# First stage of a decoder-block kernel in a written order, with aligned tiles and a sink column

## The chip, the cores and the metric

One core of one Trainium2 chip runs the whole program. The metric is the device time in microseconds (us) from launch to end, the median of the runs shown. Five engines run side by side, each in its own fixed order of instructions: PE (TensorE, the matmuls), PEld (its weight loads, shown apart), DVE (VectorE), ACT (ScalarE) and POOL (GpSimd). SP issues the DMAs. Semaphores hold an instruction until what it needs is there, and everything behind it on its engine waits with it.

## What is computed

One layer of a decoder block on 512 tokens of width 1024, in float32:

```python
h = rmsnorm(x, norm_mix)
proj = h @ w_in                       # 13 parts: q, k, v of two mixers, gates
# mixer A: window of 128 keys, and a sink logit per head in the softmax
logits = where(valid, q @ k * scale + bias, NEG)
probs = softmax(concatenate([logits, sink_col], axis=-1))[..., :span]
y_A = probs @ v
# mixer B: a compressed, a selected and a window branch, weighed by gates
x = x + (sigmoid(gA) * (y_A @ w_up_a) + sigmoid(gB) * (y_B @ w_up_b)) @ w_out
x = x + ConvFFN(rmsnorm(x, norm_ffn))
out = rmsnorm(x, norm_final)
```

## The kernel before

Every product is made of three matmuls: a float32 matrix is split in a high part (a cast, on ACT) and a low part (source minus high part, a two-input subtraction on DVE or POOL; `split`, L78), and high times high, high times low and low times high are summed (`three`, L90). A weight of 128x1024 goes through `weight` (L82): a DMA into `raw` (three buffers), the cast and the subtraction into `hl` (three buffers). The sets `POOLJ`, `U1J` and `WOP` name the weights whose subtraction is POOL's.

**First stage** (L96 to L195). The four token tiles `x` and two halves of the value weights `wvr` (816 KB each) are loaded by SP. The norm's row `nmix` is spread over the partitions by float32 matmuls into `gam`. For each tile t, `norm_x` takes two squares on ACT (L156), a sum and a scale on DVE, the power on POOL (L137), scales the tile by `r` and `gam` (L161), transposes it on PE (`tp_x`, L144), and splits it into `xTh` and `xTl`. `values(t)` sums 24 matmuls of 408 columns into `v` (L177), splits the result into `VA` and `VB`, and takes the gates. There are 96 such matmuls. The order on each engine is a scheduler's: weights of later jobs (`hl_ka`, `hl_qa`), and the bias rows `pg` (L421, for the tables `TA` and `TB`), stand between the first stage's instructions.

**Mixer A** (`unit_a`, L475; eight units: four token tiles, two groups). Per unit: four times two `scores` matmuls, a DVE pass that adds the bias from `TA` and takes the negative maximum `nma` (L449), a minimum with the negative sink (L491), four exponentials on ACT that also sum (`sma`), the sink's own exponential (`esa`, L494 and L495), its addition to the sum (L496), a reciprocal, and the scaling of `Pa` (three of four heads on POOL, L505). Then transposes (`pT`), splits (`pth`, `ptl`) and value matmuls (`oa`). Between these steps `fill` places matmuls of a queue of jobs: projections such as `p_ka`, `p_qa`, `p_ksl` (24 matmuls of 512 columns each), and the compressed branch's `h`. A job's result leaves PSUM before the second next job may start (`mm` has two banks), by DVE and ACT: `QA`, `QB`, `cx`, `KS`.

**After that** come mixer B with gate jobs `p_ga` and `p_gb` (145 to 338 us), the merge, the output projection, and the FFN (`ug`, `fo`), which is matmuls nearly alone.

`TA` is loaded from a DRAM copy `gdr` of the bias rows, which one DMA writes from 8 partitions, 32 copies each (L423).

Of the kernel before, what the change touches and what calls it, by code (L numbers as in the profile page):

```python
# [49 lines left out]
def hybrid(tc, x, wv, wblk, w1, w2, wua, wub, wout, wfi, wfo, nmix, nffn, nfin, sinks, par, table, onehot, out):  # L50
# [9 lines left out]
    with es:  # L60
        C = es.enter_context(tc.tile_pool(name="const", bufs=1))
        SL = es.enter_context(tc.tile_pool(name="slots", bufs=1))
        WR = es.enter_context(tc.tile_pool(name="wring", bufs=3))
# [39 lines left out]
        for h in range(2):  # L103
            sl = slice(h * 512, (h + 1) * 512)
            nc.sync.dma_start(xt[0][:, sl], x[0:P, sl])
            if h == 0:
                nc.sync.dma_start(grow[:, :D], nmix)
        ones = grow[:, D:]
        V.memset(ones, 1.0)
        gam = [bank("sc", f"gam{h}") for h in range(2)]  # L110
        for h in range(2):
            T.matmul(gam[h], ones, grow[:, h * 512 : (h + 1) * 512], start=True, stop=True)
# [764 lines left out]
```

## Time and profile before

| | us |
|---|---|
| median of 3 runs (770.99 to 771.98) | 771.27 |
| profiled execution, its own time | 771.21 |
| its span, first to last instruction | 769.4 |
| PE busy in the span | 747.5 (97%) |
| DVE, ACT, POOL busy | 451.0, 369.4, 156.8 |
| first matmul of `p_ka` (end of the first stage) | 38.7 |
| first matmul of `p_ga` | 145.0 |

In a row of the timeline the first number is the start in us from the span's start, the second the length; then engine, line, operation, output<-inputs, partitions x elements, a count, and in brackets the idle time of the engine before it with what ended it. PEld rows start where a matmul's weights are loaded, so four in a row give the step from matmul to matmul. In a row by stretch, each engine has its busy time and a count; behind them stand the mean granted clock of TensorE (1.00 is 2.4 GHz, 0.50 is 1.2 GHz) and the share and rate of the DMAs. In a group's row the numbers behind the bar are busy us and mean ns of one.

### The profile page before, as it was taken

The numbers are of one execution on the slowest core, as the hardware profiler recorded it, in microseconds if no ns is written. First come the engines' busy times: TensorE is split into PE (matmuls) and PEld (weight loads), VectorE is DVE, ScalarE is ACT, GpSimd is POOL, SyncE is SP. The second block draws the span as 40 slices with busy tenths as digits, with TensorE's granted clock in tenths as the row PEclk, the third lists the DMA queues.
The fourth block names the chain that finished last, engine by engine and source line by source line (L and its number), as shares of the span: only waits on it lengthen the run. The fifth ranks groups of instructions, "written<-read, shape, count | busy, mean of one in ns | idle before, by whom it ended". The sixth has DMA issues, their size and how long they took to land.

```text
span 769.4 us, 9745 instructions
## 1 busy us (share of the span) xinstructions
PE 747.5 (97%) x3590; PEld 623.3 (81%) x3590; DVE 451.0 (59%) x921; ACT 369.4 (48%) x692; POOL 156.8 (20%) x134
## 2 busy tenths in 40 slices
PE   7999989999999999999999999999999999999996
PEld 5788778788888888878889888888888888888885
DVE  5537988747655578759465665665556564214123
ACT  7345685745655856665344434343434443113213
POOL 5023536325333444402400000000000000002001
PEclk9999998999999999999999999999999999999999
DMA  8463335421112112405321323232322324232302
GB/s 304 98 148 111 108 93 169 126 83 55 56 55 83 55 60 69 145 1 192 111 78 60 109 83 110 82 110 89 104 92 101 102 90 136 85 107 85 107 28 109
DMA packets 24182, 76.74 MB, mean 100 GB/s; under 512 B 3748, under 2 KB 4900, under 8 KB 24134
## 3 DMA queue, kind: packets, MB, share of 16 engines
q1 hardware_dynamic: 24134, 76.12, 31.2%
q8 instruction: 28, 0.46, 0.3%
q14 instruction: 20, 0.16, 0.1%
HBM read 72.96 MB, written 3.15 MB: 99 GB/s over the span
## 4 chain that ended last, share of the span: by engine, by line
PE 89%; DVE 6%; issue 1%; POOL 1%; ACT 1%; DMA 1%; SPq 0%; POOLq 0%; DVEq 0%; ACTq 0%
PE ug L91 10%; PE ug L92 10%; PE ug L93 10%; PE fo L772 5%; PE fo L771 5%; PE fo L770 5%; PE pT L456 3%; PE up L91 2%; PE p_gb L91 2%; PE p_gb L92 2%; PE p_gb L93 2%; PE up L93 2%; PE up L92 2%; PE wo L91 2%; PE wo L92 2%; PE wo L93 2%
## 5 line engine op out<-in xcount | busy, mean ns | idle before, releaser
L92 PE MATMUL ug<-hTl,hl_fi 128*128 128x512 f32 (+1 forms) x376 | 141.1, 375 | 0.0
L93 PE MATMUL ug<-hTh,hl_fi 128*128 128x512 f32 (+1 forms) x376 | 141.1, 375 | 0.0
L91 PE MATMUL ug<-hTh,hl_fi 128*128 128x512 f32 (+1 forms) x376 | 140.9, 376 | 0.0
L93 PEld LDWEIGHTS ug<-hTh,hl_fi 128*128 128x128 f32 x376 | 70.8, 188 | 12.9
L91 PEld LDWEIGHTS ug<-hTh,hl_fi 128*128 128x128 f32 x376 | 70.6, 188 | 12.9
L92 PEld LDWEIGHTS ug<-hTl,hl_fi 128*128 128x128 f32 x376 | 70.8, 188 | 12.6
L754 ACT ACTIVATE cv<-ug,prm 128x512 f32<-128x512 f32 x44 | 34.3, 780 | 96.2 <-PE ug L93 96.2
L755 DVE SCALAR_TENSOR_TENSOR cv<-ug,prm,cv 128x511 f32<-128x511 f32 x44 | 33.0, 750 | 77.1 <-ACT cv L754 77.0
L771 PE MATMUL fo<-hl_fo,AH 128*128 128x512 f32 x176 | 68.8, 391 | 0.0
L770 PE MATMUL fo<-hl_fo,AH 128*128 128x512 f32 x176 | 67.3, 389 | 0.0
L796 POOL TENSOR_TENSOR X<-X,nfin 128x512 f32<-128x512 f32 x4 | 5.2, 1319 | 297.0 <-ACT junk L794 297.0
L80 DVE TENSOR_TENSOR hl_fo<-raw_fo,hl_fo 128x1024 fp32r<-128x1024 f32 x22 | 27.1, 1235 | 64.7 <-ACT hl_fo L79 64.7
L79 ACT CAST hl_fo<-raw_fo 128x1024 fp32r<-128x1024 f32 x22 | 23.1, 1052 | 65.8 <-PE fo L772 65.8
L80 DVE TENSOR_TENSOR hl_fi<-raw_fi,hl_fi 128x1024 fp32r<-128x1024 f32 x44 | 53.5, 1217 | 1.8 <-ACT hl_fi L79 1.8
L772 PE MATMUL fo<-hl_fo,AL 128*128 128x512 f32 x128 | 49.8, 389 | 0.0
L80 DVE TENSOR_TENSOR ptl<-pT,pth 128x512 fp32r<-128x512 f32 x54 | 36.5, 685 | 19.0 <-ACT pth L79 9.9
L378 ACT ACTIVATE Pb<-Pb,nmb 128x512 f32<-128x512 f32 (+3 forms) x64 | 35.9, 562 | 23.9 <-DVE nmb L449 23.6
L79 ACT CAST hl_fi<-raw_fi 128x1024 fp32r<-128x1024 f32 x44 | 45.5, 1037 | 2.4 <-PE wo L93 2.4
L79 ACT CAST pth<-pT 128x512 fp32r<-128x512 f32 x54 | 30.9, 587 | 17.7 <-PE ob L611 8.2
L771 PEld LDWEIGHTS fo<-hl_fo,AH 128*128 128x128 f32 x176 | 33.0, 188 | 7.2
L770 PEld LDWEIGHTS fo<-hl_fo,AH 128*128 128x128 f32 x176 | 33.0, 188 | 7.1
L449 DVE CUSTOM_DVE_ANT_0 Pb<-scores,TB 128x512 f32<-128x512 f32 (+3 forms) x64 | 30.7, 486 | 11.1 <-PE scores L445 9.2
(313 smaller groups left out, 1730.0 us busy)
## 6 DMA issues: line engine op xcount, KB each, us to landing
raw_fi<-in_wfi_dram SPq DMA_DIRECT2D x44, 512.0 KB, 3.3
raw_fo<-in_wfo_dram SPq DMA_DIRECT2D x22, 512.0 KB, 3.3
raw_w<-in_w_dram SPq DMA_DIRECT2D x8, 512.0 KB, 3.8
raw_ga<-in_wblk_dram SPq DMA_DIRECT2D x8, 512.0 KB, 3.3
raw_gb<-in_wblk_dram SPq DMA_DIRECT2D x8, 512.0 KB, 3.2
raw_wo<-in_wout_dram SPq DMA_DIRECT2D x5, 512.0 KB, 3.9
raw_qa<-in_wblk_dram SPq DMA_DIRECT2D x4, 512.0 KB, 4.9
raw_qb<-in_wblk_dram SPq DMA_DIRECT2D x4, 512.0 KB, 6.2
```

The lines of the kernel that those rows point to most:

```text
L79: A.copy(hi, src)
L80: (eng or V).tensor_tensor(lo, src, f(hi), op=ALU.subtract)
L91: T.matmul(ps, wh, xh, start=start, stop=False)
L92: T.matmul(ps, wh, xl, start=False, stop=False)
L93: T.matmul(ps, wl, xh, start=False, stop=stop)
L378: last_exp[0] = A.activation(a[0], a[1], AF.Exp, **k)
L449: V.tensor_tensor_reduce(ptile[:, :n], ps[:, :n], Tt[:, h, y0 : y0 + n], 1.0, HUGE, ALU.add, ALU.min, nm)
L754: A.activation(c, ps, AF.Identity, scale=cw(2, blk), bias=cb(blk))
L755: V.scalar_tensor_tensor(c[:, 1:], ps[:, : S - 1], cw(1, blk), c[:, 1:], op0=ALU.mult, op1=ALU.add)
L770: T.matmul(po[t], ah, wh, start=(k == 0), stop=False)
L771: T.matmul(po[t], ah, wl, start=False, stop=False)
L772: T.matmul(po[t], al, wh, start=False, stop=(k == NF - 1))
```

## The change

1. The first stage is written as a list, `FIRST`, and recorded under `manual_schedule`, so that each engine runs it in that order. It has four loads of value weights in place of two; POOL makes all their low parts; the norm's row is split in two parts (`gr`), and one-pass matmuls spread it. `dum1` to `dum3` are 12 matmuls on a tile of ones that nobody reads. Up to three `v` tiles are open at once (v2 in bank `o`), so value matmuls of several tiles interleave. The first weights are cast and subtracted only behind the last `xTh` and `xTl` (`issue_after`).
2. The bias rows `pg` are made with 128 output partitions, 16 copies at once, and two DMAs write `gdr` from 128 partitions.
3. POOL's share of every `split` is cut in pieces of 256 columns.
4. The sink becomes a column: `TA` has the negative sink and a column of 1e30 between its two halves, `KA` has two columns of zeros ahead of each key tile, and a unit's scores are 258 (130 for the first tile) wide. The pass that takes the maximum and the exponentials' sum then hold the sink; L491, L494, L495 and L496 go.
5. The pool `small` stands ahead of the slots and is smaller. Tiles of the pools behind it (`Pa`, `Pb`, `pth`, `ptl`, `cv`, `ALx`, `otmp`, `oy`, `pcs`, `hn`, `junk`) started 224 bytes past a multiple of 256, and start on a multiple of 256 now. The slots were there before, and are.

```diff
+FIRST = '''
+dum1 gh0 sqa0 gh1 gl0 sqb0 gl1 ga0 ms0 r0 ga1 wh00 sc00 dum2 wl00 sc01 wh01 tp00 tp01 xh00 dum3 wl01 sq1 xl00 v0010
...
-            (eng or V).tensor_tensor(lo, src, f(hi), op=ALU.subtract)
+            step = 256 if eng is G else 1 << 20
+            for c in range(0, n, step):
+                (eng or V).tensor_tensor(lo[sl], src[sl], f(hi)[sl], op=ALU.subtract)
...
+            elif what == "ms":
+                s2, m, _ = st[n[0]]
+                V.tensor_scalar(m, s2[:, 0:1], 1.0 / D, EPS, op0=ALU.mult, op1=ALU.add)
+                V.tensor_scalar(m, s2[:, 1:2], 1.0 / D, m, op0=ALU.mult, op1=ALU.add)
...
+            elif what == "wl":
+                G.tensor_tensor(wv_of(wvl, *n), wv_of(wvr, *n), f(wv_of(wvh, *n)), op=ALU.subtract)
...
+            for h in range(2):
+                for c in range(2):
+                    nc.sync.dma_start(wv_of(wvr, h, c), wv[h][:, 2 * c : 2 * c + 2])
+                if h == 0:
+                    nc.sync.dma_start(xt[1], x[P : 2 * P])
...
-                    with hp(i >= HPJ):
+                    with hp(i >= HPJ), tc.issue_after(xlast[0].ins), tc.issue_after(xlast[1].ins):
...
-        nc.sync.dma_start(gdr.rearrange("c h z -> h c z"), gsb[:, None, :].to_broadcast([8, COPIES, ZA + ZW]))
+        rows = gdr.rearrange("(u c) h z -> u (c h) z", u=2)
+        for u in range(2):
+            nc.sync.dma_start(rows[u], gsb)
...
+        V.tensor_scalar(TA[:, :, P], nsink, -1.0, None, op0=ALU.mult)
+        V.memset(TA[:, :, P + 1], 1e30)
...
-            n = P if b == 0 else 256
+            n, nk, y0 = (P + 2, 1, P) if b == 0 else (2 * P + 2, 2, 0)
...
-                V.tensor_tensor(nm, nm, ns, op=ALU.min)
...
-                V.tensor_tensor(es_, nm, ns, op=ALU.subtract)
-                exp(es_, es_)
-                V.tensor_tensor(sm, sm, es_, op=ALU.add)
```

How the order moves, at the places of which the prediction speaks. PE in the first stage, around the bias rows `pg` (before, then after; `v` are value matmuls, four or two in a row):

```order
L177 MATMUL v_172<-wvl_94,xTh_110 128x408 x4
L144 MATMUL tp_x_0_157<-ident,x_79 128x128 x4
L144 MATMUL tp_x_1_165<-ident,x_79 128x128 x4
L177 MATMUL v_232<-wvh_91,xTh_109 128x408 x4
L144 MATMUL tp_x_0_217<-ident,x_80 128x128 x4
L421 MATMUL pg_418<-og,tab 8x384
L421 MATMUL pg_421<-og,tab 8x512
L144 MATMUL tp_x_1_225<-ident,x_80 128x128 x4
L177 MATMUL v_232<-wvh_91,xTl_111 128x408 x4
```

```order
L228 MATMUL v_188<-wvl_86,xTh_91 128x408 x2
L209 MATMUL tp_x_1_230<-ident,x_75 128x128 x4
L250 MATMUL pg_236<-og,gx 128x384
L250 MATMUL pg_238<-og,gx 128x512
L250 MATMUL pg_240<-og,gx 128x128
L228 MATMUL v_253<-wvh_83,xTl_92 128x408 x2
L228 MATMUL v_188<-wvl_86,xTh_91 128x408 x2
L228 MATMUL v_253<-wvh_83,xTh_90 128x408 x2
L228 MATMUL v_253<-wvl_85,xTh_90 128x408 x2
```

Before, 28 value matmuls stand ahead of `pg` and 68 behind; now 20 and 76, with all three `pg` matmuls together, and the last transposes of tiles 2 and 3 follow among the 76.

ACT in the first stage, from the middle of the value weights' casts (before, then after; `s2x` are the squares' sums):

```order
L79 CAST wvh_92<-wvr_90 128x1632
L156 ACTIVATE junk_207,s2x_206<-x_80 128x512
L156 ACTIVATE junk_209,s2x_206<-x_80 128x512
L156 ACTIVATE junk_266,s2x_265<-x_80 128x512
L156 ACTIVATE junk_268,s2x_265<-x_80 128x512
L79 CAST VA<-v_172 128x2x64
L79 CAST hl_ka<-raw_ka 128x1024
L79 CAST xTh_109<-tp_x_0_157 128x4x128
L79 CAST VB<-v_172 128x4x64
L79 CAST xTh_110<-tp_x_1_165 128x4x128
L79 CAST hl_qa_368<-raw_qa_366 128x1024
```

```order
L215 CAST xTh_90<-tp_x_0_164 128x4x128
L195 ACTIVATE junk,s2x_182<-x_75 128x512 x2
L219 CAST wvh_84<-wvr_82 128x816
L215 CAST xTh_91<-tp_x_1_169 128x4x128
L219 CAST wvh_84<-wvr_82 128x816
L195 ACTIVATE junk,s2x_217<-x_76 128x512 x2
L215 CAST xTh_90<-tp_x_0_212 128x4x128
L195 ACTIVATE junk,s2x_245<-x_76 128x512 x2
L215 CAST xTh_91<-tp_x_1_230 128x4x128
L253 COPY og<-pg_236 128x384
L253 COPY og<-pg_238 128x512
L253 COPY og<-pg_240 128x128
```

The casts of `hl_ka` and `hl_qa` have left the stretch, and the copies of the bias rows stand behind the fourth pair of squares and one more `xTh`.

DVE in mixer A, where the third unit's scores are finished while `p_qa` (the fourth query block) is taken out of PSUM (before, then after):

```order
L491 TENSOR_TENSOR nma<-nma,nsink 128x4
L494 TENSOR_TENSOR esa<-nma,nsink 128x4
L333 SCALAR_TENSOR_TENSOR QA_708<-p_qa_762,QA_708 64x512
L470 TENSOR_TENSOR oy<-oa,otmp 64x256 x2
L80 TENSOR_TENSOR ptl<-pT,pth 128x512 x2
L449 ISA Pa,nma<-scores,TA 128x256
L449 ISA nma 128x1
L496 TENSOR_TENSOR sma<-sma,esa 128x4
```

```order
L583 RECIPROCAL sma<-sma 128x4
L593 TENSOR_SCALAR Pa<-Pa,sma 128x258
L94 TENSOR_TENSOR ptl<-pT,pth 128x512 x2
L425 SCALAR_TENSOR_TENSOR QA_748<-p_qa_800,QA_748 64x512
L540 ISA Pa,nma<-scores,TA 128x258
L540 ISA nma 128x1
```

The three 128x4 operations with the sink are gone, and nothing stands in their place.

POOL in mixer A, from the first weight job behind `ka` (before, then after):

```order
L80 TENSOR_TENSOR hl_kc<-raw_kc,hl_kc 128x1024
L80 TENSOR_TENSOR hl_qa_512<-raw_qa_510,hl_qa_512 128x1024
L80 TENSOR_TENSOR hl_w_0_0_613<-raw_w_0_0_611,hl_w_0_0_613 128x1024
L80 TENSOR_TENSOR hl_qa_715<-raw_qa_713,hl_qa_715 128x1024
L505 TENSOR_TENSOR Pa<-Pa,sma 128x128 x3
```

```order
L94 TENSOR_TENSOR hl_kc<-raw_kc,hl_kc 128x256 x4
L94 TENSOR_TENSOR hl_qa_556<-raw_qa_554,hl_qa_556 128x256 x4
L94 TENSOR_TENSOR hl_w_0_0_655<-raw_w_0_0_653,hl_w_0_0_655 128x256 x4
L94 TENSOR_TENSOR hl_qa_755<-raw_qa_753,hl_qa_755 128x256 x4
L591 TENSOR_TENSOR Pa<-Pa,sma 128x130 x3
```

The order is the same, and each weight's subtraction is four instructions instead of one.

## Rows read from the trace of the kernel before

**Rows 1.** By stretch: length; PE, PEld, DVE, ACT, POOL busy (count); clock; DMA.

```profile
7.90:38.70 30.80, 28.26 (x134) 24.50 (x135) 20.35 (x38) 16.79 (x37) 9.60 (x10) 0.94 0.66 186
...
80.00:90.40 10.40, 9.14 (x50) 7.15 (x48) 10.17 (x24) 6.51 (x17) 6.15 (x6) 1.00 0.31 101
90.40:94.60 4.20, 4.20 (x12) 3.30 (x13) 4.16 (x9) 2.27 (x4) 3.19 (x2) 0.59 0.35 126
...
111.60:115.50 3.90, 0.25 (x3) 0.06 (x2) 3.80 (x4) 3.04 (x11) 3.03 (x2) 0.90 0.78 179
115.50:122.00 6.50, 6.48 (x22) 5.58 (x23) 5.29 (x19) 2.27 (x8) 3.62 (x3) 0.53 0.92 297
122.00:145.00 23.00, 21.81 (x117) 18.18 (x115) 19.49 (x40) 17.93 (x40) 12.87 (x11) 1.00 0.51 128
145.00:330.00 185.00, 184.74 (x966) 155.31 (x967) 119.83 (x384) 111.51 (x254) 73.29 (x56) 1.00 0.22 73
```

**Rows 2.** Timeline of the first stage, ACT, POOL and PE.

```profile
7.32 1.55 ACT L79 CAST wvh<-wvr 128x1632 fp32r<-128x1632 f32 x1 [1.30 <-DMA wvr<-in_wv_dram]
8.95 3.67 POOL L80 TENSOR_TENSOR wvl<-wvr,wvh 128x1632 fp32r<-128x1632 f32 x1 [1.91 <-ACT wvh L79]
9.04 0.59 ACT L79 CAST xTh<-tp_x 128x512 fp32r<-128x512 f32 x1 [0.16 <-PE tp_x L144]
...
13.43 0.60 ACT L156 ACTIVATE junk<-x 128x512 f32<-128x512 f32 x1
...
14.19 0.60 ACT L156 ACTIVATE junk<-x 128x512 f32<-128x512 f32 x1
...
20.99 1.68 PE L421 MATMUL pg<-og,tab 33*8 33x384 f32 x4 [1.67 <-DVE x L161]
...
21.84 0.47 ACT L422 COPY og<-pg 8x384 f32<-8x384 f32 x1 [1.83 <-PE pg L421]
```

**Rows 3.** Loads of the token tiles 2 and 3, by line: starts, and time to landing.

```profile
L120 SPq DMA_DIRECT2D x<-in_x_dram x2: 514/622/729, 3.4 to 4.1; - x2
...
DMA to landing us min/median/max: 8.6/8.8/9.1
```

**Rows 4.** Timeline of PEld, late in the first stage: step from matmul to matmul.

```profile
24.54 1.35 PEld L177 LDWEIGHTS v<-wvh,xTh 128*128 128x128 f32 x4
...
28.70 0.54 PEld L144 LDWEIGHTS tp_x<-ident,x 128*128 128x128 f32 x4
...
34.05 0.75 PEld L177 LDWEIGHTS v<-wvh,xTh 128*128 128x128 f32 x4
```

**Rows 5.** Timeline in mixer A: two POOL weights, two DVE operations, PE's next matmul.

```profile
109.95 2.38 POOL L80 TENSOR_TENSOR hl_w<-raw_w,hl_w 128x1024 fp32r<-128x1024 f32 x1
...
110.77 1.58 DVE L491 TENSOR_TENSOR nma<-nma,nsink 128x4 f32<-128x4 f32 x1
...
112.29 2.35 POOL L80 TENSOR_TENSOR hl_qb<-raw_qb,hl_qb 128x1024 fp32r<-128x1024 f32 x1
112.38 2.27 DVE L494 TENSOR_TENSOR esa<-nma,nsink 128x4 f32<-128x4 f32 x1
...
115.52 0.55 PE L275 MATMUL h<-hl_w,XX 128*128 128x256 f32 x1 [3.67 <-DVE QB L333]
```

**Rows 6.** Groups on DVE, 43 to 145 us: busy us, mean ns.

```profile
L494 DVE TENSOR_TENSOR esa<-nma,nsink 128x4 f32<-128x4 f32 x8 | 6.0, 745 | 0.2
...
L491 DVE TENSOR_TENSOR nma<-nma,nsink 128x4 f32<-128x4 f32 x8 | 5.5, 687 | 0.1
...
L496 DVE TENSOR_TENSOR sma<-sma,esa 128x4 f32<-128x4 f32 x8 | 1.3, 160 | 3.8 <-ACT esa L378 3.8
```

**Rows 7.** A group on POOL, 43 to 340 us: busy us, mean ns.

```profile
L599 POOL TENSOR_TENSOR Pb<-Pb,smb 128x256 f32<-128x256 f32 x8 | 5.2, 671 | 12.1 <-ACT Pb L378 8.8 <-DVE smb L574 3.3
```

**Rows 8.** Groups on PE, FFN's second product: aligned AL, shifted ALx; mean ns.

```profile
L772 PE MATMUL fo<-hl_fo,AL 128*128 128x512 f32 x128 | 49.8, 389 | 0.0
...
L772 PE MATMUL fo<-hl_fo,ALx 128*128 128x512 f32 x48 | 18.9, 394 | 0.0
```

More of the change, by code (lines that the diff above doesn't have):

```diff
@@ L102, in hybrid @@
         xt = [(x01, x23)[t // 2][:, t % 2] for t in range(NT)]
[L103 to L112, printed above, removed]
+        halves = [slice(0, 512), slice(512, 1024)]
+        gx = slot(6, [33, D + 256 + 16], F32, "gx")
+        grow, tab = gx[:1, :D], gx[:, D + 256 :]
+        tabc = gx[:, D : D + 256].rearrange("p (b c h) -> p b c h", b=2, h=8)
+        gr = slot(14, [1, 2, D], F32R, "gr")
+        og = slot(15, [P, 2, ZA + ZW], F32, "og")
+        oh, gsb = og[:33, 0], og[:, 1]
+        nsink = SM.tile([P, 8], F32, tag="n8", name="nsink", bufs=1)
         wvr = [slot(7 + h, [P, 4, NV], F32, f"wvr{h}") for h in range(2)]
@@ L188, in hybrid @@
-        norm_x(0)
-        VA = slot(16, [P, NT, 2, P], F32R, "VA")
-        for h in range(2):
-            split(wvh[h], wvl[h], wvr[h], (G, None)[h])
-        for t in range(1, NT):
-            norm_x(t)
-            values(t - 1)
-        values(NT - 1)
+        VA = slot(16, [P, NT, 2, P], F32R, "VA")
+        one = VA.rearrange("p t n d -> p (t n d)")[:, :512]
+        junk = WR.tile([P, D], F32, tag="raw", name="junk", bufs=RAW)
+        first = FIRST.split()
+        st, ps_v, tp_x, out_v = {}, {}, {}, {}
@@ new lines, in hybrid, with wv_of, busy, out_of @@
+        pgs = ((0, ZA, 0), (ZA, ZA + 512, 1), (ZA + 512, ZA + ZW, 1))
+        def wv_of(w, h, c):
+            return w[h][:, 2 * c : 2 * c + 2]
+        def busy(n):
+            for i in range(n):
+                T.matmul(bank("mm", "idle"), one[:, :P], one, start=True, stop=True)
+        def out_of(t):
+            if t not in out_v:
+                ps = ps_v[t][:, 0:384].rearrange("p (n d) -> p n d", d=64)
+                out_v[t] = ps[:, 0:2], ps[:, 2:6], SM.tile([P, 24], F32, tag="eg", name=f"eg{t}", bufs=2)
+            return out_v[t]
@@ new lines, in hybrid @@
+        xlast, pgs_t = [None, None], []
+        with tc.manual_schedule():
+            V.memset(f(one), 1.0)
+            V.memset(warm[:, 0:1], 0.0)
+            V.memset(mhalf, -0.5)
+            make_identity(nc, ident)
+            G.memset(tab, 1.0)
+            nc.scalar.dma_start(grow, nmix)
+            A.activation(warm[:, 0:1], warm[:, 0:1], AF.Exp)
+            for h in range(2):
+                nc.sync.dma_start(xt[0][:, halves[h]], x[0:P, halves[h]])
+            for h in range(2):
+                for c in range(2):
+                    nc.sync.dma_start(wv_of(wvr, h, c), wv[h][:, 2 * c : 2 * c + 2])
+                if h == 0:
+                    nc.sync.dma_start(xt[1], x[P : 2 * P])
+            for t in range(2, NT):
+                nc.sync.dma_start(xt[t], x[t * P : (t + 1) * P])
+            nc.sync.dma_start(tab[:32], table)
+            nc.sync.dma_start(oh, onehot)
+            nc.sync.dma_start(prm, par)
+            nc.sync.dma_start(nsink, bc(sinks, 8))
+            gam = [bank("sc", f"gam{h}") for h in range(2)]
+            for u in first:
+                do(u)
@@ L213, in filler @@
         def filler():
-            i, nxt = 0, jobs[0][1]()
+            with tc.issue_after(xlast[0].ins), tc.issue_after(xlast[1].ins):
+                i, nxt = 0, jobs[0][1]()
             while nxt is not None:
@@ L763, in hybrid @@
         nc.sync.dma_start(NFN, bc(nfin, D))
-        s2s = [SM.tile([P, 2], F32, tag=f"s3_{t}", name=f"s3_{t}", bufs=1) for t in range(NT)]
+        s3 = SM.tile([P, 8], F32, tag="n8", name="s3", bufs=1)
+        s2s = [s3[:, 2 * t : 2 * t + 2] for t in range(NT)]
         def fo_mm(po, t, hl, kk, k):
```

190 lines of the change are left out of this document (113 added, 77 removed).

## Prediction

> **What bounds the kernel now.** I read the busy time by stretch first. From 145 us on PE is the bound: in 145 to 330 us it is busy for 184.74 of 185.00 us at the full clock [rows 1], and the FFN behind it is matmuls end to end, so what a change can win there lies in the step from matmul to matmul. What is not PE's own time lies ahead of 145 us, in two parts.
>
> The first stage ends when `p_ka` starts, at 38.7 us. In 7.9 to 38.7 us PE idles 30.80 − 28.26 = 2.5 us, and the mean granted clock is 0.94 [rows 1]: some 12% of the time is at 1.2 GHz, 3.7 us, of which half is lost, 1.9 us. The step shows it: four value matmuls take 0.75 us at 34.05 but 1.35 us at 24.54 [rows 4]. At the short steps, 96 value matmuls (0.75/4 each) and 32 transposes (0.54/4 each) would take 18.0 + 4.3 us, and `pg` 1.7 us [rows 2, 4]: 24 of the 30.8 us. So some 7 us of the stage are waits and slow steps.
>
> Mixer A has three episodes [rows 1]. E1: PE idles 1.26 us of 80 to 90.4, then runs 4.2 us at clock 0.59, where 82% of the time is at 1.2 GHz and half of that, 1.7 us, is lost; together 3.0 us. E2: PE works 0.25 of 3.90 us (111.6 to 115.5), then 6.5 us at clock 0.53, where 3.0 us are lost; together 6.7 us. E3: 1.2 us idle in 122 to 145. The sum is 10.9 us.
>
> The cause of E2 stands in the timeline [rows 5]. L491, a 128x4 operation on DVE, starts at 110.77 and ends at 112.35, as POOL's `hl_w` does (109.95 + 2.38 = 112.33). L494 starts at 112.38 and ends at 114.65, as POOL's `hl_qb` does (112.29 + 2.35 = 114.64). Behind these two stands the DVE half of `QB`, and for that PE waits 3.67 us. Eight of L494 take 745 ns in the mean and eight of L491 687, against 160 for L496, of the same size [rows 6]. So here a DVE operation that reads two tiles in SBUF does not end before POOL's running subtraction has. [...]
>
> **The change, part by part.** The sum is made against the profiled execution's own 771.21 us (span 769.4 and 1.8 around it), 0.06 below the median of 771.27.
>
> *First stage.* I walk the new order with the old durations. The loads keep their bytes and their order, so the last two token tiles land as now, at 3.4 + 8.6 = 12.0 and 4.1 + 9.1 = 13.2 us [rows 3]. ACT is the chain. The second quarter of the value weights lands where the first half did, at 7.3; its cast, half of 1.55, ends at 8.1, and `xTh` of tile 0 (0.6) at 8.8 [rows 2]. Then come the squares of tile 1 at 0.76 each (14.19 − 13.43), to 10.3; a weight cast to 11.1; `xTh` to 11.7; a weight cast to 12.5; the squares of tile 2 to 14.0; `xTh` to 14.6; the squares of tile 3 to 16.2; `xTh` to 16.8; and the first bias copy (0.47) to 17.3 [rows 2]. For that copy PE waits with the third `pg` matmul, since `pt` has three banks, and all else on PE waits behind it, until 17.6 with this matmul. POOL's four low parts (3.67/2 each) end near 15.1, and its powers for tiles 2 and 3 near 15.7 and 18.8, ahead of PE's need.
>
> From 17.6 PE has 76 value matmuls and 16 transposes: 76 × 0.1875 + 16 × 0.135 = 14.3 + 2.2 us. `p_ka` starts at 34.0 and not at 38.7. Its weight is now cast behind the last `xTh`, near 29, and its first quarter on POOL is ready near 31; value matmuls hide it, and if it came after 34, each us late would cost one. Gain **4.7 us**. Bounds: 2.8, if the stage keeps the 1.9 us that the low clock costs it now, and 6.8, if no wait is left (30.8 − 24). The norm row's split and its matmuls lie under the load of tile 0's second half, and the dummies end before `gam` can start. If either were late, the scaling of tile 0 would be, by as much.
>
> Four loads of value weights could cost more than two. In the trace they stand in a full queue, and I take none. [...]
>
> *Sink column.* It takes 24 small operations off DVE, 6.0 + 5.5 + 1.3 us [rows 6], and eight small exponentials off ACT. In E2 they hold 1.58 + 2.27 us [rows 5], about the idle 3.65 us, and the low clock came behind the idle, in E1 too. Other two-input operations stay, but a hold is then one quarter: a POOL operation of 256 columns takes 0.67 us [rows 7]. Two more columns in 64 score matmuls cost 64 × 2 × 0.46 ns, 0.06 us. So E1 gives back 2.5 of 3.0, E2 6.2 of 6.7 and E3 half of 1.2, 9.3 us. Late next is DVE again, which takes `p_vc` and the query blocks out in bursts; I leave 1.0 us to that. Gain **8.3 us**, bounds 3 (new bursts take the rest) and 10.9 (all three episodes).
>
> *Quarters on POOL.* A weight of 2.38 us becomes four pieces of at most 0.67, 2.7 us [rows 5, 7]. A job of 24 matmuls with 512 columns covers it: at 512/408 of a value matmul's step they take 5.6 us [rows 4], and POOL is busy 73 of the 185 us from 145 on [rows 1]. **0**; uncovered, 0.3 us for each weight.
>
> *Bias table.* The copy in DRAM is written near 18 us by 128 partitions, and the table still waits for the last value matmul. The scores come three jobs later, 16.8 us, which hides its eight loads. **0**; a late table would cost what it is late.
>
> *Aligned tiles.* The same matmul takes 389 ns with `AL` and 394 with the shifted `ALx` [rows 8]. 5 ns each for 48 of these and some 110 on `pth` and `ptl` give **0.7 us**, bounds 0 and 0.8.
>
> The sum is 771.2 − 4.7 − 8.3 − 0.7 = **757.5 us**. The bounds of the terms give 771.2 − 2.8 − 3 − 0 = 765.4 and 771.2 − 6.8 − 10.9 − 0.8 = 752.7.
>
> **The rivals.** *R1, the clock falls in the first stage.* Between 14.5 and 17.6 PE stands still twice, for some 1.3 us in all, around the `pg` matmuls; in E1 1.26 us of idle were followed by 4.2 us at clock 0.59 [rows 1]. Against it, value matmuls run ahead of this place, and in E1 mostly single transposes that waited. At the 1.9 us of now the time is 759.4. [...]
>
> *R2, new bursts in mixer A.* The scheduler has set the evictions anew, and the gain there may be its lower bound of 3 to 4 us. Against it, DVE loses 12.8 us of work in a part that it filled only in the episodes (10.17 of 10.40 us in E1) [rows 1, 6]. It gives 762.5.
>
> *R3, the order does not shorten the first stage.* `pg` stands ahead of 76 value matmuls. If its operands, loaded behind tile 3 at 13.2 [rows 3], come some 4 us later than I think, `p_ka` stays near 38.7, and the time is 762.2. Against it, they are 134 KB.
>
> *R4, slower.* POOL's quarters have to get past DVE's two-input operations one by one, as DVE's past POOL's. If a weight's four pieces then take more than the 5.6 us of its job, POOL becomes the bound from 145 to 330 us, where some 18 of its 56 instructions are weights. At 6.6 us that costs 18 us, so 775.5; 5.6 us is the point from which it decides, and above 6.4 us the whole gain is gone. Against it, POOL has 60% of that time free [rows 1].
>
> **How the numbers follow.** A measurement of this kernel cannot tell 0.2% (1.5 us) from no change. The forecast, 754 to 759, has 0.58; R1 0.14; R2 0.14; R3 0.07; R4 0.04; and 0.03 is left for less than 752.5. The range of 752.5 to 766 takes in the bounds and R1 to R3. Faster 0.93; same 0.03, half of it R4 at a low price and half R2 and R3 together; slower 0.04.
>
> **What would show it.** The first `p_ka` matmul at 33 to 35 us, with the first copy of `pg` near 17 and PE standing still just ahead of it; no 128x4 operation on DVE over 1 us ahead of 145 us; PE without a gap of 1 us and with a clock near 1.00 from there to the first `p_ga` matmul, which starts near 132 (145.0 − 4.7 − 8.3); 389 ns with `ALx`; pieces of 0.6 to 0.7 us on POOL. `p_ka` later than 36 makes the walk wrong, and a clock under 0.9 between 80 and 120 us the sink's term.

## The result, and the profile after

| | us |
|---|---|
| kernel before, median of the runs shown with this result | 771.62 |
| changed kernel, median of 4 runs (762.31 to 764.42) | 763.86 |
| ratio, with its 95% interval | 0.9900 (0.9879 to 0.9922) |
| profiled execution of the changed kernel, and its span | 764.42, 762.6 |
| forecast (range) | 757.5 (752.5 to 766.0) |

The kernel is faster by 7.8 us, between 6.0 and 9.3 by the interval. The forecast was 13.7. The direction and the range hold; six of the 13.7 us are missing. The busy time by stretch of the changed kernel, in the columns of [rows 1]:

```profile
7.90:36.66 28.76, 25.97 (x138) 23.32 (x137) 18.13 (x36) 16.97 (x41) 14.56 (x17) 1.00 0.55 199
36.66:43.00 6.34, 6.34 (x21) 5.04 (x22) 1.61 (x9) 0.10 (x1) 0.00 (x0) 0.73 1.05 265
...
91.00:97.00 6.00, 4.79 (x23) 3.83 (x22) 5.12 (x13) 2.92 (x8) 5.76 (x7) 1.00 0.29 87
97.00:108.00 11.00, 10.16 (x57) 8.68 (x56) 9.62 (x26) 9.24 (x23) 2.11 (x3) 1.00 0.36 104
...
122.00:131.40 9.40, 7.70 (x41) 6.43 (x40) 6.57 (x12) 7.42 (x12) 4.63 (x7) 1.00 0.95 272
145.00:330.00 185.00, 184.51 (x974) 155.48 (x973) 112.42 (x381) 110.90 (x253) 79.96 (x114) 1.00 0.22 72
```

The first stage now has clock 1.00, not 0.94 as in [rows 1], and ends at 36.66 us, not at 38.7. But behind it comes a stretch at clock 0.73, where there was none before. Behind 43 us no stretch of mixer A is at a low clock any more, while PE still idles 1.2 us in 91 to 97, 0.8 us in 97 to 108 and 1.7 us in 122 to 131.4. From 145 us on PE is the bound as before, and POOL is far from it with 80 of 185 us.

Three signs of the forecast came true or nearly so: POOL's pieces, DVE's 128x4 operations, and the time of a matmul with `ALx`. By group (busy us, mean ns of one):

```profile
L94 POOL TENSOR_TENSOR hl_w<-raw_w,hl_w 128x256 fp32r<-128x256 f32 x20 | 14.4, 753 | 6.6 <-ACT hl_w L88 6.6
```

```profile
L583 DVE RECIPROCAL sma<-sma 128x4 f32<-128x4 f32 x8 | 1.4, 176 | 0.8 <-ACT Pa L477 0.7
```

```profile
L858 PE MATMUL fo<-hl_fo,AH 128*128 128x512 f32 x176 | 68.5, 389 | 0.0
...
L859 PE MATMUL fo<-hl_fo,ALx 128*128 128x512 f32 x48 | 18.7, 389 | 0.0
```

A quarter of `hl_w` takes 753 ns in the mean, against the 0.6 to 0.7 us of the forecast. The reciprocal is the only 128x4 operation left on DVE in mixer A, at 176 ns. `ALx` takes 389 ns, as `AL` does, and not 394 [rows 8].

The first `p_ga` matmul starts at 131.6 us, as if the 132 of the forecast were met. That sign was misread: 145.0, from which the 132 was counted, is where the second such job starts in the profile of before. The first starts at 136.0 there, right behind `p_kw` as in the changed kernel, so it came 4.4 us earlier. From the profile of before:

```profile
L91 PE MATMUL p_ga<-xTh,hl_ga x64: 389/389/504, 136.0 to 216.2; 128*128 128x512 f32 x64
```

The first scores against `KS`, which stand behind the whole of mixer A, come 6.6 us earlier, near the gain of the whole profiled execution (771.21 to 764.42, 6.8 us). Before, and after (shortest, median and longest in ns, first and last start):

```profile
L444 PE MATMUL scores<-KS,QB x32: 235/348/477, 165.0 to 325.5; 128*128 128x512 f32 x8, 128*128 128x416 f32 x8, 128*128 128x288 f32 x8, 128*128 128x160 f32 x8
```

```profile
L535 PE MATMUL scores<-KS,QB x32: 234/350/483, 158.4 to 318.9; 128*128 128x512 f32 x8, 128*128 128x416 f32 x8, 128*128 128x288 f32 x8, 128*128 128x160 f32 x8
```

So most of the gain, and what is missing of it, lies ahead of 160 us.

### The profile page after: what moved, and what is told of

It reads as the page before. It is cut to its first block, busy times and chain, and to the rows that moved or that the text cites. A ratio compares the mean times of both kernels' runs of the same rounds, so it can differ in the third digit from the quotient of the medians.

```text
span 762.6 us, 9931 instructions
## 1 busy us (share of the span) xinstructions
PE 744.4 (98%) x3602; PEld 623.1 (82%) x3602; DVE 427.6 (56%) x902; ACT 368.2 (48%) x686; POOL 183.5 (24%) x258
## 4 chain that ended last, share of the span: by engine, by line
PE 87%; DVE 5%; ACT 3%; DMA 2%; issue 2%; POOL 0%; SPq 0%; POOLq 0%; DVEq 0%; ACTq 0%
PE ug L105 11%; PE ug L106 11%; PE ug L107 10%; PE fo L857 5%; PE fo L859 5%; PE fo L858 5%; PE pT L547 2%; PE up L105 2%; PE p_ga L105 2%; PE p_ga L106 2%; PE p_ga L107 2%; PE up L107 2%; PE up L106 2%; PE wo L107 2%; PE wo L106 2%; PE wo L105 2%
```

## Experiments on the first stage

What stands at its end in the changed kernel, on PE, DVE and POOL:

```profile
30.88 4.79 POOL L94 TENSOR_TENSOR hl_ka<-raw_ka,hl_ka 128x256 fp32r<-128x256 f32 x4 [3.69 <-ACT hl_ka L88]
...
31.79 3.30 DVE L94 TENSOR_TENSOR hl_qa<-raw_qa,hl_qa 128x1024 fp32r<-128x1024 f32 x2 [1.21 <-ACT hl_qa L88]
...
33.55 1.28 PE L228 MATMUL v<-wvh,xTh 128*128 128x408 f32 x6
35.01 0.69 DVE L242 TENSOR_SCALAR eg<-eg 128x24 f32<-128x24 f32 x1
...
36.23 0.28 DVE L233 TENSOR_TENSOR VA<-v,VA 128x128 fp32r<-128x128 f32 x1
...
36.66 0.47 PE L105 MATMUL p_ka<-xTh,hl_ka 128*128 128x512 f32 x1 [1.84 <-DVE eg L242]
```

The last value matmuls start at 33.55 and take six steps, to 34.7: the walk said 34.0. Then PE waits for 2.0 us. `p_ka` takes the PSUM bank of the value tile `v1`, and DVE takes `v1` out (35.01 to 36.51) only behind the low parts of two `hl_qa` weights, 3.30 us in a row. The change had moved these there, behind the last `xTl`. What `p_ka`'s first matmul reads was ready: it takes the high part of `hl_ka`, whose cast ended at 30.8. And the two subtractions last long: POOL's four pieces of `hl_ka` lie beside them, at 4.79 us where four times 0.75 would be 3.0.

**a_la1: these low parts behind `v1`'s last subtraction**

```diff
-                V.tensor_tensor(VA[:, n[0], :, 64:128], out_of(n[0])[0], f(VA[:, n[0], :, 0:64]), op=ALU.subtract)
+                lal[n[0]] = V.tensor_tensor(VA[:, n[0], :, 64:128], out_of(n[0])[0], f(VA[:, n[0], :, 0:64]), op=ALU.subtract)
...
-                    with hp(i >= HPJ), tc.issue_after(xlast[0].ins), tc.issue_after(xlast[1].ins):
+                    with hp(i >= HPJ), tc.issue_after(xlast[0].ins), tc.issue_after(lal[1].ins):
```

> The changed kernel with one edit: the low parts of the later weights on DVE (two of hl_qa first) stand behind la1, the last subtraction that takes the tile v1 out of PSUM, instead of ahead of it. In the profile of the changed kernel the value matmuls end at 34.6 us, p_ka waits to 36.66 for v1's bank, and the clock is 0.73 until 43. Theory A (the wait is v1's eviction behind two hl_qa subtractions, and the low clock follows from the wait): p_ka starts at 34.6 to 35.0, the clock stays near 1.00, and the time falls by 2.0 + 1.7 us, to about 760.2. Theory B (p_ka waits as long for its own weight, whose low part POOL finishes at 35.7, or for something else that lies beside it): p_ka stays at 36 or later and the time within 1 us of 763.9.

760.76 us (759.23 to 763.54), ratio 0.9864 (0.9827 to 0.9902). The same place in its profile, and the stretch behind it:

```profile
30.06 2.84 POOL L94 TENSOR_TENSOR hl_ka<-raw_ka,hl_ka 128x256 fp32r<-128x256 f32 x4 [3.69 <-ACT hl_ka L88]
...
32.73 1.27 PE L228 MATMUL v<-wvh,xTh 128*128 128x408 f32 x6
...
33.05 2.35 DVE L94 TENSOR_TENSOR hl_qa<-raw_qa,hl_qa 128x1024 fp32r<-128x1024 f32 x2
...
33.84 0.39 PE L105 MATMUL p_ka<-xTh,hl_ka 128*128 128x512 f32 x1
```

```profile
34.70:43.00 8.30, 8.30 (x38) 6.85 (x38) 3.70 (x12) 3.03 (x5) 1.13 (x2) 1.00 1.06 249
```

Theory A holds: `p_ka` starts at 33.84, right behind the last value matmul, the clock is 1.00, and the median is 3.1 us lower (expected 3.7; the intervals of the two medians overlap, so this size is rough). Apart from each other, DVE's two subtractions take 2.35 us and POOL's four pieces 2.84.

**a_dum9: nine idle matmuls in PE's wait**

```diff
             for u in first:
                 do(u)
+            for i in range(9):
+                T.matmul(bank("sc", "idle2"), xTh[0][:, 0, :P], xTh[0][:, 0], start=True, stop=True)
```

> The changed kernel with nine matmuls of 512 columns, which nobody reads, ahead of p_ka, in a bank that is free; they fill the 2 us in which PE waits there. Theory A (the low clock from 37.7 to 43 comes from the idle time ahead of it): p_ka still starts near 36.7, but the clock stays near 1.00 and the time falls by about 1.5 us, to 762.3. Theory B (the clock falls for another reason): the clock near 0.73 again and the time at 763.9; if the nine last longer than the wait, up to 0.5 us more.

763.58 us (762.37 to 764.89). This one settles little. The clock behind `p_ka` was 1.00, as theory A has it, but only five of the nine stood ahead of `p_ka`; the other four came among the matmuls of `p_ka` and `p_qa` and cost 0.9 us there. And in its profiled execution the low clock was elsewhere, between 18 and 24 us (0.50 in 20 to 22), so that `p_ka` started at 37.9.

**b_rest: all of the change but the first stage.** The kernel before, with the diffs of the sink column, of the quarters and of the pools. Its first stage has the order of the kernel before.

> The kernel before with the sink column, POOL in quarters and aligned tiles, so all of the change but the first stage and the bias table. Theory A (the new first stage ends 2.0 us earlier but loses 1.7 us of it to the low clock behind p_ka's wait, so it is worth some 0.4 us, and the rest of the change 7.4): p_ka at 38.7, time 764.3. Theory B (the first stage is worth its 4.7 us, and the other parts fell short): about 768.5.

763.66 us (762.52 to 764.80), ratio 0.9890 (0.9862 to 0.9917): as fast as the whole change, to within the some 2 us of the intervals. So the new first stage, with the wait for `v1` in it, is worth nothing that can be measured. The rows of its first stage:

```profile
7.90:36.70 28.80, 26.98 (x134) 23.05 (x135) 18.53 (x40) 17.22 (x37) 10.27 (x15) 1.00 0.71 202
```

```profile
36.73 0.40 PE L95 MATMUL p_ka<-xTh,hl_ka 128*128 128x512 f32 x1
```

The old order, at clock 1.00, brings `p_ka` to 36.73 us. In the profile of before it was at 38.7 with a clock of 0.94 [rows 1], so most of these 2.0 us were the low clock of that execution (1.9 us by the forecast's count), not the order. The new order has its value matmuls done 2.1 us earlier, and the wait for `v1` gives just that back. Without the wait, in a_la1, `p_ka` starts 2.9 us ahead of this one (33.84 against 36.73), both at clock 1.00.

**a_pg: the bias rows later.** PE also stands still at `pg`, which the forecast's rivals R1 and R3 were about. In the profile of the changed kernel:

```profile
12.36 3.84 POOL L221 TENSOR_TENSOR wvl<-wvr,wvh 128x816 fp32r<-128x816 f32 x2
...
14.62 1.73 DVE L247 COPY gx<-gx 33x256 f32<-33x256 f32 x1 [0.18 <-DMA gx<-in_table_dram]
...
16.40 2.32 PE L250 MATMUL pg<-og,gx 33*128 33x384 f32 x6 [0.88 <-DVE ssqx L198]
```

The operands of `pg` were there in time (DVE's copy of the table's rows waited only 0.18 us for their load). But this copy of 33x256, at 14.62, took 1.73 us and ended at 16.35, POOL's two `wvl` at 16.20. These are 1.9 us each: the first stage does not go through `split`, and its POOL work is not cut. The run is made on the kernel of a_la1kw (below), in `FIRST`:

```diff
-v0000 v0021 v0020 wh10 ms1 v0011 r1 v0001 xh01 wl10 sc10 wh11 v0100 xl01 tp10 sq2 sc11 v0101 v0121 wl11 v0110 tp11 pg
-xh10 ms2 sq3 xl10 r2 sc21 v1020 xh11 sc20 v0111 pgc xl11 v1000 ms3 v1011 r3 sc30 v1111 v1100 sc31 v1120 tp20 v1021
+v0000 v0021 v0020 wh10 ms1 v0011 r1 v0001 xh01 wl10 sc10 wh11 v0100 xl01 tp10 sq2 sc11 v0101 v0121 wl11 v0110 tp11
+xh10 ms2 sq3 xl10 r2 sc21 v1020 xh11 sc20 v0111 xl11 v1000 ms3 v1011 pg r3 sc30 v1111 pgc v1100 sc31 v1120 tp20 v1021
```

> The kernel of the run with la1 and the table's loads moved, and the three pg matmuls (with the copy of the table's rows on DVE) some ten matmuls later on PE; the copies of pg stand on ACT where they did. In that run PE lost 1.1 us at 14.9 us waiting for pg's operands and 1.1 us within pg, and ran at 1.2 GHz from 18.5 to 22, which cost 1.7 us; other executions (the changed kernel's profile) had the same waits and no low clock. Theory A (the forecast's rival R1: PE's standing still around pg brings the low clock there): clock 1.00 in 16 to 34 us, p_ka 1 to 2.5 us earlier, median 757.5. Theory B (the low clock comes from elsewhere, or the wait only moves to the transposes of tile 2): 759.1.

761.61 us (759.05 to 762.71), ratio 0.9862 (0.9838 to 0.9886), not faster than a_la1kw. Theory B: the wait only moved. The copy now stands behind tile 3's mean (`ssqx`), comes at 19.26, and PE waits 1.67 us for it:

```profile
19.26 0.28 DVE L249 COPY gx<-gx 33x256 f32<-33x256 f32 x1
...
19.59 1.77 PE L252 MATMUL pg<-og,gx 33*128 33x384 f32 x4 [1.67 <-DVE gx L249]
```

Here no POOL subtraction runs beside the copy (POOL is idle from 17.12 to 19.42 us), and it takes 0.28 us.

**The low clock of the first stage.** Between 18 and 26 us it came in some profiled executions of the new order and not in others. The changed kernel itself was profiled twice (after2 is the same program, below); first the first profile, then after2:

```profile
18.00:24.00 6.00, 6.00 (x34) 5.59 (x33) 4.15 (x10) 1.80 (x5) 0.68 (x2) 1.00 0.65 259
```

```profile
18.00:24.00 6.00, 6.00 (x24) 5.30 (x23) 3.36 (x7) 1.04 (x4) 0.68 (x2) 0.72 0.68 257
...
36.00:44.00 8.00, 6.16 (x21) 4.74 (x20) 4.06 (x15) 0.62 (x3) 1.50 (x1) 0.79 0.92 256
```

The traces of before and after have the clock at 1.00 or 0.50 and at nothing between; 0.72 is a mean of the two. At 0.50 the weights of `p_ksl`'s matmuls are loaded 0.43 us apart, and 0.23 at 1.00; from the profile of before, by stretch and on PEld:

```profile
91.00:94.00 3.00, 3.00 (x9) 2.33 (x8) 2.97 (x7) 1.67 (x4) 2.59 (x2) 0.50 0.47 173
```

```profile
91.84 0.33 PEld L93 LDWEIGHTS p_ksl<-xTh,hl_ksl 128*128 128x128 f32 x1
92.27 0.33 PEld L91 LDWEIGHTS p_ksl<-xTh,hl_ksl 128*128 128x128 f32 x1
92.69 0.33 PEld L92 LDWEIGHTS p_ksl<-xTl,hl_ksl 128*128 128x128 f32 x1
...
94.34 0.19 PEld L93 LDWEIGHTS p_ksl<-xTh,hl_ksl 128*128 128x128 f32 x1
94.58 0.19 PEld L91 LDWEIGHTS p_ksl<-xTh,hl_ksl 128*128 128x128 f32 x1
94.80 0.19 PEld L92 LDWEIGHTS p_ksl<-xTl,hl_ksl 128*128 128x128 f32 x1
```

With 512 columns each these are 1.2 columns a ns at 0.50, the prediction's 1.2 GHz (the 1.35 us of [rows 4] for four times 408 give the same), and some 2.2 at 1.00, a little less than twice as many; so near half of the time at 0.50 is lost. At 0.72 over 6 us, half of 3.4 us is lost, 1.7 us. This is R1 with its price, and it comes and goes. Of the twelve profiles of the new first stage, six had it: a_dum9, a_la1kw, a_swap, after2, a_pg and a_all. In five of these PE stood still behind 8 us until the first `wvl` was there (busy 0.91 to 1.52 of the 2.00 us from 8 to 10), and in a_all for 1.6 us around `pg` (busy 2.41 of the 4.00 us from 16 to 20); in the other six it did neither (busy for all of 8 to 10 us, and idle for at most 1.0 us from 14 to 18). That is a coincidence of rows; no run was made to separate it.

## Experiments on mixer A

The sink column and the quarters were each taken back alone.

**a_nosink: without the sink column**

```diff
-            n, nk, y0 = (P + 2, 1, P) if b == 0 else (2 * P + 2, 2, 0)
+            n, nk, y0 = (P, 1, P) if b == 0 else (256, 2, 0)
...
+                V.tensor_tensor(nm, nm, ns, op=ALU.min)
...
+                V.tensor_tensor(es_, nm, ns, op=ALU.subtract)
+                exp(es_, es_)
+                V.tensor_tensor(sm, sm, es_, op=ALU.add)
```

> The changed kernel without the sink column: the 24 small operations on DVE and 8 exponentials are back, all else is as in the changed kernel. Theory A (with POOL in quarters a hold is short, and most of what was lost in mixer A was DVE's bursts of evictions): no 128x4 operation over 1.2 us, time 763.9 + 2 to 4, so 766 to 768. Theory B (the sink's operations are the 8.3 us of the forecast): 771 to 773.

767.41 us (765.60 to 770.91), ratio 0.9946 (0.9924 to 0.9968): 3.5 us more than the changed kernel, in the range of theory A. The sink's operations on DVE with POOL in quarters, in the columns of [rows 6]:

```profile
L584 DVE TENSOR_TENSOR esa<-nma,nsink 128x4 f32<-128x4 f32 x8 | 3.1, 387 | 0.2
...
L581 DVE TENSOR_TENSOR nma<-nma,nsink 128x4 f32<-128x4 f32 x8 | 2.1, 257 | 0.2
```

They take 387 and 257 ns in the mean, against 745 and 687 ns [rows 6]: the quarters halve the holds, and the column takes away the rest. But the 3.5 us are mostly not these operations' time. The waits of PE over 0.25 us, from `p_ka` to the first scores against `KS`, add up to 2.8 us here and to 4.6 in the changed kernel. What this profile has more are two stretches at low clock, each worth up to 1.7 us, and the second lies where no operation of the sink stands:

```profile
122.00:127.00 5.00, 5.00 (x18) 3.96 (x17) 4.45 (x10) 2.56 (x7) 5.00 (x8) 0.66 0.40 116
333.00:339.00 6.00, 4.30 (x14) 3.40 (x14) 1.26 (x3) 4.87 (x8) 0.00 (x0) 0.72 0.00 0
```

All ten executions have a mean clock of 0.987 to 0.993, the four of the changed kernel 0.995 to 0.997. The scheduler also placed the jobs anew without the column, so this run does not show how much is the column's own.

**a_whole: POOL's subtractions whole**

```diff
-            step = 256 if eng is G else 1 << 20
+            step = 1 << 20
```

> The changed kernel with POOL's subtractions whole again (2.4 us each for a weight) and the sink column kept. The order of the later jobs moves with it in places. Theory A (quarters matter also without the sink's operations, since YA, XX and ptl on DVE read two tiles in SBUF and POOL's Pa waits too): one to three holds of up to 2.4 us come back in mixer A, time 763.9 + 1.5 to 3.5, so 765.4 to 767.4. Theory B (the holds were the sink's operations alone, as in the forecast's sum, where quarters alone count as 0): within 1 us of 763.9.

764.96 us (764.43 to 765.37), ratio 0.9918 (0.9895 to 0.9942): 1.1 us more, so between the two theories, and the intervals overlap. The profiles agree with a small loss: from the first `p_ka` matmul to the first scores against `KS` it is 123.4 us here and 121.8 in the changed kernel, each with one stretch at low clock. Holds come back on operations that have nothing to do with the sink. `hp` and `YA` on DVE, in the changed kernel and then in a_whole:

```profile
L564 DVE TENSOR_TENSOR YA<-oy,YA 128x256 fp32r<-128x256 f32 x7 | 3.9, 551 | 0.0
...
L376 DVE TENSOR_TENSOR hp<-cx,hb 62x256 f32<-62x256 f32 x2 | 1.0, 496 | 0.9 <-issue 0.9
```

```profile
L564 DVE TENSOR_TENSOR YA<-oy,YA 128x256 fp32r<-128x256 f32 x7 | 5.6, 805 | 0.5 <-ACT YA L563 0.5
...
L376 DVE TENSOR_TENSOR hp<-cx,hb 62x256 f32<-62x256 f32 x2 | 2.6, 1302 | 0.8 <-PE pT L547 0.7
```

What is left in the changed kernel are three waits of PE: for `p_vc`'s eviction (`cx`), for `h`'s, and for `QB`'s and `h`'s together.

```profile
90.13 2.26 DVE L348 TENSOR_TENSOR cx<-p_vc,prm 64x248 f32<-64x248 f32 x6
...
92.54 0.47 PE L105 MATMUL p_ksl<-xTh,hl_ksl 128*128 128x512 f32 x1 [1.21 <-DVE cx L348]
```

```profile
102.58 0.50 PE L105 MATMUL p_qb<-xTh,hl_qb 128*128 128x512 f32 x1 [0.84 <-ACT cx L367]
```

```profile
122.18 1.05 ACT L88 CAST hl_kw<-raw_kw 128x1024 fp32r<-128x1024 f32 x1 [2.58 <-DMA raw_kw<-in_wblk_dram]
...
123.26 1.23 DVE L94 TENSOR_TENSOR hl_kw<-raw_kw,hl_kw 128x1024 fp32r<-128x1024 f32 x1 [2.69 <-ACT hl_kw L88]
...
125.24 0.42 DVE L369 TENSOR_TENSOR cx<-cx,h 128x256 f32<-128x256 f32 x1
...
125.81 0.47 PE L105 MATMUL p_kw<-xTh,hl_kw 128*128 128x512 f32 x1 [1.70 <-DVE cx L369]
```

The first is E1, where PE idled 1.26 us [rows 1], 0.96 of them ahead of `p_ksl`. In the profile of before:

```profile
87.24 3.00 DVE L260 TENSOR_TENSOR cx<-p_vc,prm 64x248 f32<-64x248 f32 x8
...
90.38 0.47 PE L91 MATMUL p_ksl<-xTh,hl_ksl 128*128 128x512 f32 x1 [0.96 <-DVE cx L260]
```

PE waited for the last of eight `cx` operations in a row, and it does so now, for 1.21 us; the sink's operations were not what it waited for. In the third, DVE waits with `hl_kw`, whose weight landed late, and `QB` and `cx` stand behind it.

**a_la1kw: the table's loads behind `raw_kw`**, on the kernel of a_la1.

```diff
             TB.append(slot((11, 10)[g], [P, 4, 512], F32, f"TB{g}"))
-            toeplitz(TB[g], 4 * g, 4, ZA, 512)
             if g:
+                toeplitz(TB[g], 4 * g, 4, ZA, 512)
                 gates_a()
             need(*(("ksl", "qb0", "qb1", "kw", "h1_03", "h1_13"), ("qb2", "qb3"))[g])
+            if not g:
+                with tc.issue_after(dm["kw"].ins):
+                    toeplitz(TB[g], 4 * g, 4, ZA, 512)
```

> The kernel of the run with the low parts behind la1, and the loads of the table TB of group 0 behind the load of raw_kw on SP's queue, where they stood ahead of it. Theory A (the gap of 1.4 to 1.9 us ahead of p_kw near 119 to 124 us comes from raw_kw, which landed 7.25 us after its issue beside the table's loads, and holds DVE's queue): the gap falls under 0.4 us, the time by 1.2 to 1.5 us against the run with la1 alone, to about 759.4. Theory B (the gap is DVE's burst of QB and cx, whatever raw_kw does): the gap and the time, 760.8, stay.

759.13 us (758.39 to 759.92), ratio 0.9843 (0.9819 to 0.9867): 1.6 us under a_la1 (the intervals overlap), theory A. PE does not wait for `p_kw` any more:

```profile
121.62 0.47 PE L107 MATMUL p_kw<-xTh,hl_kw 128*128 128x512 f32 x1
```

This is the fastest kernel of the study: 4.7 us under the changed kernel, and 11.7 under the median of before on the same chip (770.85).

**a_swap: a long job behind `p_vc`**, on a_la1kw.

```diff
-AORD = 'ka qa0 qa1 kc qa2 h00 qa3 h01 vc h02 ksl h10 qb0 h11 h03 h12 qb1 h13 kw'
+AORD = 'ka qa0 qa1 kc qa2 h00 qa3 h01 vc ksl h02 h10 qb0 h11 h03 h12 qb1 h13 kw'
```

> The kernel of the run with la1 and the table's loads moved, and in the list of mixer A's jobs p_ksl (24 matmuls) ahead of h02 (8 matmuls), so that behind p_vc there is a long job in the other bank while DVE takes p_vc out in eight operations. Theory A (the gap of 1.4 us ahead of p_ksl, which was there before the change too, is p_vc's eviction, not the sink's operations): the gap near 87 us goes, and the time is 758 to 759, unless h10 behind h02 now waits as long. Theory B (the gap has another cause): it moves along with p_ksl or h02 unchanged, 759.4.

761.63 us (759.82 to 762.53), ratio 0.9872 (0.9846 to 0.9899): slower by 2.5 us. The wait ahead of `p_ksl` went, as theory A has it, and came back as 1.31 us ahead of the next `h` at 97.5 us, behind `KS`'s two subtractions and `h02`'s addition on DVE. So it was `p_vc`'s eviction, and the order of the jobs only chooses whose eviction PE waits for. Why the median rose by more than these waits, this run does not tell; its profile has the low clock of the first stage too, as that of a_la1kw has.

**a_all: evictions ahead of other work**, on a_pg.

```diff
-                evac(ps)
+                with hp(i_evac(name)):
+                    evac(ps)
...
+                with tc.high_priority():
                     if b == 0:
                         A.copy(ac, ph[:, :256])
```

> The kernel of the run before, and the operations that take the projections and h out of PSUM recorded with high priority, so that the scheduler puts them ahead of other work on DVE and ACT (p_vc's eight operations then stand in a row, ahead of the next scores' pass); the order in mixer A moves with it. Theory A (the gaps of 1.4 and 1.0 us that are left in mixer A come from what stands ahead of the evictions, so their order decides): PE's gaps between 80 and 122 us fall from 3.5 to under 2 us, time 1 to 2 us under the run with pg later. Theory B (DVE has as much work there as time, and the wait goes elsewhere, to the scores or pT): the same time within 0.7 us, or up to 1 us more.

766.35 us (764.53 to 768.97), ratio 0.9931 (0.9908 to 0.9954). By stretch, a_la1kw and then a_all:

```profile
80.00:122.00 42.00, 39.77 (x231) 34.21 (x230) 35.66 (x93) 31.39 (x74) 30.36 (x43) 1.00 0.48 137
...
260.00:340.00 80.00, 78.08 (x406) 65.53 (x405) 57.36 (x171) 48.23 (x107) 30.58 (x43) 1.00 0.22 71
```

```profile
80.00:122.00 42.00, 40.92 (x234) 35.14 (x233) 36.52 (x93) 32.13 (x74) 30.07 (x44) 1.00 0.49 151
...
260.00:340.00 80.00, 75.46 (x381) 61.69 (x380) 52.53 (x175) 46.15 (x109) 30.51 (x44) 0.96 0.20 67
```

In 80 to 122 us PE idles 1.1 us and no longer 2.2 (a_pg, from which the edit starts, has 2.2 and 1.9 us of idle time in the two stretches, as a_la1kw): theory A is right there, the order of the evictions decides. But the scheduler placed mixer B anew as well, and in 260 to 340 us PE idles 4.5 us and not 1.9, at clock 0.96. The gain is more than given back, in a place the edit was not about.

## Experiments on the aligned tiles

**a_misal and a_misal2: the pool 224 bytes off, and after2: the changed kernel beside it.** Every instruction stands in the same order.

```diff
+        es.enter_context(tc.tile_pool(name="pad", bufs=1)).tile([P, 56], F32, name="pad")
         ea = contextlib.ExitStack()
```

> The changed kernel with an unused tile of 224 bytes ahead of the pool of Pa, pth, ptl and ALx, so that these start 224 bytes past a multiple of 256 as before; every instruction stands where it did. Theory A (the forecast's 0.7 us): fo with ALx at 394 ns again, 764.6. Theory B (alignment does nothing): ALx at 389 ns, 763.9.

> The changed kernel as it is, on the same chip as the next run, for a comparison of the two. All theories: 763.9, or 0.990 of the kernel before.

> The changed kernel with the pool of Pa, pth, ptl and ALx 224 bytes past a multiple of 256, a second time, beside the changed kernel. The profiles of the first run show the steps longer by 0.4 us for fo with AH, 0.2 with ALx, 0.2 each for up with YA, ob and p_ga, some 1.3 us in all, where the forecast had 0.7; the medians stood 2.3 us apart. Theory A (the steps are all there is): 1.0 to 1.5 us over the changed kernel on the same chip. Theory B (the alignment also costs elsewhere, or lengthens the stretches at low clock): 2 us or more.

| | us, median | ratio |
|---|---|---|
| a_misal (5 runs) | 766.16 | 0.9942 (0.9919 to 0.9965) |
| after2 (6 runs) | 765.08 | 0.9917 (0.9888 to 0.9946) |
| a_misal2 (6 runs) | 764.03 | 0.9908 (0.9884 to 0.9932) |

By the medians nothing can be said: 2.3 us against the changed kernel the first time, −1.0 the second. The executions of one program differ by up to 5 us here, since the low clock comes in some and not in others (in after2 their mean clocks go from 0.989 to 0.997). The single matmuls are steadier. In a_misal2, by group:

```profile
L859 PE MATMUL fo<-hl_fo,AH 128*128 128x512 f32 x176 | 68.8, 391 | 0.0
...
L860 PE MATMUL fo<-hl_fo,ALx 128*128 128x512 f32 x48 | 18.9, 394 | 0.0
```

`ALx` takes 394 ns again [rows 8], and `AH` 391, against 389 and 389 above. `ALx` is the operand that is loaded as weights here, in blocks of 128x128; the 512 columns that move past it are `hl_fo`'s. The `AH` matmuls that are longer are those right ahead of an `ALx` one: 396 ns, with 235 ns to the next start and not 227; all others stay at 389.

From the first scores against `KS` to the end of the last matmul, with the same instructions in between and no low clock, both profiles of the changed kernel take 597.3 us, and the two with the pool off 598.5 and 598.4. So aligned tiles give 1.2 us, of which 0.4 are the `AH` matmuls ahead of `ALx`. The kernel before takes 597.7 us for this stretch, only 0.4 more than the changed kernel. One `p_ga` matmul more, 0.2 us, stands in it now; what else takes the rest back there, no run shows.

## Why the prediction was right, and where not

The measured time lies in the range because the range takes in R2 and R3; the forecast's own 754 to 759 was missed by 4.9 us.

**What bounds the kernel: right.** PE from 145 us on, and two places ahead of it. Behind 160 us the profiles of before and after differ by 0.2 to 0.4 us.

**First stage, 4.7 us forecast, 0 measured (b_rest against the changed kernel). This is the step that failed.** The walk over the new order held: value matmuls done at 34.7 in the changed kernel and 33.8 in a_la1, for a forecast of 34.0. Tile 3 landed 1.1 us later than in the walk: issued at 5.2 us and not at 4.1, and there 9.1 us later, as before [rows 3], at 14.3; the stage hid it. Two steps of this term were wrong:

- "Its weight is now cast behind the last `xTh`, near 29, and its first quarter on POOL is ready near 31; value matmuls hide it." That was true of `hl_ka` and of POOL. The same edit had moved the low parts of two `hl_qa` to the same place on DVE, ahead of the evictions of `v1`, and `p_ka` takes `v1`'s bank. The walk followed who makes the operands of `p_ka` and left out who frees its bank. a_la1 shows the price: 3.1 us by the medians; in the profile the wait was 2.0 us and the low clock behind it up to 1.7.
- The 38.7 us from which the 4.7 were counted held 1.9 us of low clock, and the forecast took them for the order's. b_rest, with the same order, had none. Its lower bound of 2.8 left them in the new stage, when they should have been left out of the old one.

**Sink column, 8.3 us forecast, some 6.9 for it and the quarters together.** b_rest gains 8.1 us (771.74 to 763.66) without the first stage, and the 6.9 are what is left of these without the 1.2 of the aligned tiles. Its profile has 120.1 us from `p_ka` to the first scores against `KS`, that of before 126.3. The mechanism was right for E2: its 3.65 us of idle time are gone, and with them the low clock. What was mis-sized is "I leave 1.0 us" for the evictions that are late next: the three waits are 1.21 + 0.84 + 1.70 = 3.75 us. The episodes' 10.9 us less 3.75 are 7.2, near the 6.9. E1 was read wrongly. PE's idle time there was put down to the sink's operations; 0.96 of its 1.26 us were `p_vc`'s eviction, and this wait is 1.21 us now. E1 gave back its low clock only. So rival R2 came true in part. What the column gives without the quarters stays open. The forecast's 0.46 ns for a column are the 0.75/4 us of [rows 4] over 408 columns.

**Quarters on POOL, 0 forecast: perhaps too little.** Taken out alone they cost 1.1 us (a_whole), within the overlap of the intervals. That they cost nothing from 145 us on was right: POOL has 105 of 185 us free from 145 us on, so R4 did not come. But what R4 rests on was seen, on a small scale: beside DVE's whole `hl_qa` four pieces took 4.79 us, and 2.84 without (a_la1).

**Bias table, 0: right.** No wait for `TA` was seen; what `pg` costs PE, 0.88 us of waiting at 15.5, is in the walk as 1.3 us around `pg`. The cause was another: not the third `pg` matmul's bank alone, but a copy on DVE that took 1.73 us beside POOL's `wvl`, and 0.28 in a_pg.

**Aligned tiles, 0.7 us forecast (0 to 0.8), 1.2 measured.** The matmul ahead of one with a shifted `ALx` is longer too, and `AH`'s were not counted. Of the 1.2 the whole change shows only 0.4 behind 160 us.

**The rivals.** R3 came true in its result (the first stage not shortened) and not in its mechanism: `pg`'s operands were there. R1 came in half of the profiles, R2 in part, R4 not.

**The sign at `p_ga`: misread.** Counted from the first such matmul of before, at 136.0, it would have been 123.0 and not 132; measured is 131.6.

The sum of what was measured, 0 + 6.9 + 1.2 = 8.1 us, is b_rest's gain by the way it was made, so that it is near 7.8 is no check of the parts. Taken out one by one, the column, the quarters and the alignment cost 3.5 + 1.1 + 1.2 = 5.8 us.

## What to carry to other kernels

When a step is moved, list what each of its instructions passes on every engine, and for the first matmul behind it ask two things: who makes its operands, and who empties the bank it writes. Before a low-clock stretch in one profile is put into a sum, see whether another execution, or an unchanged stage of another kernel, has it too. And where one engine empties many banks, as DVE does here, count its evictions, rather than leave a round number for them: with E2's stall gone, three waits for them were left, 3.75 us.
